# A two-layer diffusion backbone with eight experts: loading pairs of expert weight units only as pairs

## Chip, cores and metric

The kernel runs on one core of a Trainium2 chip. The metric is the device time of one execution in microseconds (us); the median of several runs is compared.

## What is computed

256 latent tokens and 256 context tokens of width 1024 pass through two layers: layer 0 is neighbourhood attention and a dense SwiGLU, layer 1 a two-way linear recurrence and a SwiGLU with eight experts, of which every token uses two. All inputs are fp32. The change touches the loading of the expert weights:

```python
def moe_ffn(h, w_router, b_router, w1, w3, w2):
    logits = (h @ w_router).astype(jnp.float32) + b_router.astype(jnp.float32)
    top_v, top_i = lax.top_k(logits, TOP_K)          # TOP_K = 2 of N_EXPERTS = 8
    gates = jax.nn.softmax(top_v, axis=-1)
    ...
    for e in range(N_EXPERTS):                       # D_FF_EXPERT = 3584
        y = y + comb[..., e:e + 1] * swiglu(h, w1[e], w3[e], w2[e])
```

Each expert has three matrices of 1024x3584 fp32, together 44 MB, and all eight are read once: 352 MB of the 490 MB that the whole kernel moves.

## The kernel before

**Units.** Weights come as units of 128x1024 fp32 (512 KB), in one list, in the order in which they are used. An expert is seven steps of 512 hidden columns. A step uses four units of w1, four of w3 (`up`, `small_up`) and, one step later, four of w2 (`w2_step`): 84 units an expert, 672 for all; only the last four (`w2c`, from `w2l`) are laid out otherwise. The host lays two neighbouring units side by side, so that a partition's 2x1024 values are 8 KB in one piece; the even unit of such a pair has a second way to be read, `both` (`add_moe`), which fetches the pair in one transfer of 1024 KB.

**Heavy and light experts.** Experts are sorted by their number of tokens. Places 0, 2, 4, 6 are heavy: ScalarE cuts each unit to a high part (`whi`, line 345), VectorE makes the low part (`wlo`, line 356), and TensorE does three matmuls of 512 columns for each product (lines 1871 to 1873 and 1804 to 1806). A heavy unit's place is free as soon as `wlo` is written. Places 1, 3, 5, 7 (`LIGHT`) have few tokens and use the raw fp32 units in TensorE (line 1784, called by `pair`); such a unit's place is free only when its matmuls are done.

**Places.** `Raws.homes` is a list of pools. Single places hold one unit (the pool `raw`, three of them; one more for a while), double places hold two (`wide`: four in `hp`, two in `rawm`, one in `raw3`, up to three in `zp`): 10 double and 3 single places for most of the expert stage. `load` is called whenever a place becomes free. It issues, on SyncE's queue (SP), as many loads as there are free places, strictly in the order of the list. A load waits on SP for the last reader of the place it writes. The expert's number is read from memory into a register of SP, since the order of the experts is data.

**How `load` chooses before.** If the next unit begins a pair and a double place is wholly free, it issues one transfer of 1024 KB (line 273). Otherwise it takes the first place that is free or half filled and issues the unit alone, 512 KB (line 289). A pair's first unit may thus fill a single place or the second half of a double place; the second unit of the pair has no `both` and is then always loaded alone, and it may open a double place whose other half the next pair's first unit fills. A double place is given back when both of its halves are used.

Of the kernel before, what the change touches and what calls it, by code (L numbers as in the profile page):

```python
# [241 lines left out]
class Raws:  # L242
# [18 lines left out]
    def add(self, key, ap, both=None):  # L261
        self.units.append((key, ap, both))

    def load(self, n=100):
        while self.dma_at < len(self.units) and n:
            n -= 1
            i = self.dma_at
            _, ap, both = self.units[i]
            r = next((r for r in self.homes if r.wide and r.free()), None) if both else None
            if r:  # L270
                b = r.block()
                b[1] = 2
                self.nc.sync.dma_start(b[0], both())
                self.raws[i], self.raws[i + 1] = (b[0][:, 0], b), (b[0][:, 1], b)
                self.dma_at += 2
                continue
            r = next((r for r in self.homes if r.part or r.free()), None)
            if r is None:
                return
            if r.part:  # L280
                b, t, r.part = r.part, r.part[0][:, 1], None
                b[1] += 1
            else:
                b = r.block()
                b[1] = 1
                t = b[0][:, 0] if r.wide else b[0]
                if r.wide:
                    r.part = b
            self.nc.sync.dma_start(t, ap() if callable(ap) else ap)
            self.raws[i] = (t, b)  # L290
            self.dma_at += 1

    def head(self):
        return self.units[self.at][0] if self.at < len(self.units) else None
# [100 lines left out]
def body(tc, nc, es, a, out, upto, dbg):  # L395
# [1548 lines left out]
    def overflow(p):  # L1944
# [38 lines left out]
        for s in range(NST):  # L1983
            acc = [psa("ph"), psa("ph")]
            for part in range(2):
                for i in range(4):
                    w = load(s, 4 * part + i)
                    for kk in range(2):
                        k = 2 * i + kk
                        nc.tensor.matmul(  # L1990
                            acc[part], xo[:, k], w[:, kk * 512:kk * 512 + 512], start=(k == 0), stop=(k == KD - 1)
                        )
            sil = mp.tile([P, 512], F32, name="msil", tag="msil", bufs=1)
            nc.scalar.activation(sil, acc[0], AF.Silu)
            nc.vector.tensor_tensor(sil, sil, acc[1], ALU.mult)
            g = pst("pgt")
            for i in range(4):
                nc.tensor.transpose(g[:, i * P:i * P + P], sil[:, i * P:i * P + P], ident)
            go = mp.tile([P, 512], F32, name="msil", tag="msil", bufs=1)
            nc.scalar.copy(go, g)  # L2000
            for f in range(4):
                w = load(s, 8 + f)
                for n in range(2):
                    nc.tensor.matmul(
                        yo[n], go[:, f * P:f * P + P], w[:, n * 512:n * 512 + 512],
                        start=(s == 0 and f == 0), stop=(s == NST - 1 and f == 3),
                    )
# [38 lines left out]
```

## Time and profile before

| | us |
|---|---|
| median of 3 runs | 1856.36 (1855.66 to 1859.17) |
| the profiled execution, its own time | 1857.41 |
| its span, first to last instruction | 1855.5 |
| TensorE busy | 1771.2 (95%) |
| VectorE busy | 1185.9 (64%) |
| ScalarE busy | 860.5 (46%) |
| chain that ended last: TensorE / DMA / VectorE | 71% / 13% / 10% |

The span is what the trace covers; 1.9 us of the execution's time lie around it. Busy time of TensorE counts matmuls whose ends are modelled, so 95% does not mean that it is at its limit everywhere. The 40 slices of the page are 46.4 us each; the expert stage begins in slice 22, counted from 1.

### The profile page before, as it was taken

What the parts mean: (1) busy time and instruction counts of PE and PEld (TensorE: products, weight loads), DVE (VectorE), ACT (ScalarE), POOL (GpSimd) and SP (SyncE); (2) the same over time, 40 slices, a digit from 0 to 9 for tenths busy, and PEclk for the clock granted to TensorE, in tenths of its full rate; (3) what the DMA queues carried; (4) which work ended last, traced back from release to release, by engine and by line L of the source; (5) the groups of instructions that cost most, each with busy time, mean ns of one, the idle gap of its engine ahead of it and who ended that gap; (6) DMA issues with size and microseconds to landing.
All of it is one profiled execution on the core that took longest, in us unless ns stands there. A gap on an engine that the chain in (4) does not pass through costs nothing.

```text
span 1855.5 us, 27189 instructions
## 1 busy us (share of the span) xinstructions
PE 1771.2 (95%) x10067; PEld 1351.2 (73%) x10067; DVE 1185.9 (64%) x1751; ACT 860.5 (46%) x1263; POOL 188.4 (10%) x195
## 2 busy tenths in 40 slices
PE   8999999999999999999778999999998999999996
PEld 6886568988788888877667885578655886478753
DVE  4784676877665447699988862288515972089611
ACT  4534655422222235776736761277314762067500
POOL 1001342100000002344640000000000000000000
PEclk8999999999999999999888999999999999999999
DMA  7444611464655223232566889999999999999996
GB/s 304 162 158 137 217 46 46 164 219 156 232 210 185 96 79 117 80 111 85 214 253 212 325 300 406 412 412 414 416 414 412 412 414 410 413 410 412 414 414 270
DMA packets 118588, 489.96 MB, mean 264 GB/s; under 512 B 13104, under 2 KB 18608, under 8 KB 100528
## 3 DMA queue, kind: packets, MB, share of 16 engines
q1 hardware_dynamic: 118304, 488.02, 69.1%
q8 instruction: 81, 1.33, 0.3%
q14 instruction: 59, 0.48, 0.1%
q10 hardware_dynamic: 144, 0.13, 0.0%
HBM read 487.05 MB, written 1.05 MB: 263 GB/s over the span
## 4 chain that ended last, share of the span: by engine, by line
PE 71%; DMA 13%; DVE 10%; ACT 3%; issue 1%; POOL 1%; SPq 0%; DVEq 0%; ACTq 0%; POOLq 0%
DMA raw<-moe_d 12%; PE ph L1784 6%; PE ph L1873 5%; PE ph L1871 5%; PE ph L1872 5%; PE psa L445 4%; PE psa L446 4%; PE psa L447 4%; PE py L1804 3%; PE py L1806 3%; PE py L1805 3%; PE py L1784 3%; DVE wlo L356 2%; PE pF L445 2%; PE pF L446 2%; PE pF L447 2%
## 5 line engine op out<-in xcount | busy, mean ns | idle before, releaser
L356 DVE TENSOR_TENSOR wlo<-raw,whi 128x1024 fp32r<-128x1024 f32 x480 | 575.4, 1234 | 158.1 <-ACT whi L345 154.7
L345 ACT CAST whi<-raw 128x1024 fp32r<-128x1024 f32 x484 | 491.5, 1048 | 207.0 <-PE pF L446 49.8
L1784 PE MATMUL ph<-raw,xs 128*64 128x256 f32 x1792 | 210.2, 383 | 9.1 <-DMA raw<-moe_d 8.8
L1873 PE MATMUL ph<-wlo,xe 128*128 128x512 f32 x448 | 177.3, 396 | 6.9 <-DVE wlo L356 6.8
L1871 PE MATMUL ph<-whi,xe 128*128 128x512 f32 x448 | 179.4, 400 | 2.2 <-ACT whi L345 2.2
L1784 PEld LDWEIGHTS ph<-raw,xs 128*64 128x64 f32 x1792 | 122.5, 137 | 76.3 <-DMA raw<-moe_d 13.6
L1872 PE MATMUL ph<-whi,xe 128*128 128x512 f32 x448 | 176.2, 393 | 0.0
L445 PE MATMUL psa<-hh,whi 128*128 128x512 f32 (+1 forms) x384 | 144.7, 377 | 0.0
L446 PE MATMUL psa<-hl,whi 128*128 128x512 f32 (+1 forms) x384 | 143.7, 374 | 0.7 <-DVE hl L696 0.6
L447 PE MATMUL psa<-hh,wlo 128*128 128x512 f32 (+1 forms) x384 | 143.2, 373 | 0.0
L1901 DVE TENSOR_TENSOR msil<-msil,ph 128x256 f32<-128x256 f32 x28 | 11.8, 420 | 155.7 <-PE ph L1784 155.7
L1784 PE MATMUL py<-raw,mgs 128*64 128x512 f32 (+1 forms) x496 | 104.6, 557 | 3.9 <-DMA raw<-moe_d 3.3
L1873 PEld LDWEIGHTS ph<-wlo,xe 128*128 128x128 f32 x448 | 85.2, 190 | 28.7 <-DVE wlo L356 10.3
L570 DVE SCALAR_TENSOR_TENSOR macc<-raw,c,macc 128x1024 f32<-128x1024 f32 x84 | 105.2, 1279 | 0.6
L1871 PEld LDWEIGHTS ph<-whi,xe 128*128 128x128 f32 x448 | 85.0, 190 | 19.2 <-ACT whi L345 2.9
L1872 PEld LDWEIGHTS ph<-whi,xe 128*128 128x128 f32 x448 | 85.3, 190 | 17.0
L1804 PE MATMUL py<-whi,mgh 128*128 128x512 f32 x224 | 87.6, 391 | 0.0
L1806 PE MATMUL py<-wlo,mgh 128*128 128x512 f32 x224 | 87.3, 390 | 0.0
L1805 PE MATMUL py<-whi,mgl 128*128 128x512 f32 x224 | 87.2, 389 | 0.0
L445 PEld LDWEIGHTS psa<-hh,whi 128*128 128x128 f32 x384 | 73.0, 190 | 14.3 <-issue 2.1
L446 PEld LDWEIGHTS psa<-hl,whi 128*128 128x128 f32 x384 | 73.0, 190 | 13.7 <-DVE hl L696 1.5
L447 PEld LDWEIGHTS psa<-hh,wlo 128*128 128x128 f32 x384 | 72.9, 190 | 12.5
(351 smaller groups left out, 3231.8 us busy)
## 6 DMA issues: line engine op xcount, KB each, us to landing
raw<-moe_d SPq DMA_DIRECT2D x388, 512.0 KB, 10.8
raw<-moe_d SPq DMA_DIRECT2D x140, 1024.0 KB, 14.1
raw<-f_d SPq DMA_DIRECT2D x66, 512.0 KB, 3.6
raw<-wm_d SPq DMA_DIRECT2D x64, 512.0 KB, 4.6
raw<-wmh_d SPq DMA_DIRECT2D x32, 512.0 KB, 7.5
raw<-qkv_d SPq DMA_DIRECT2D x24, 512.0 KB, 4.2
raw<-win_d SPq DMA_DIRECT2D x24, 512.0 KB, 3.6
raw<-gat_d SPq DMA_DIRECT2D x14, 512.0 KB, 3.7
```

The costliest lines, as they stand in the source:

```text
L345: self.nc.scalar.copy(hi, self.raws[i][0])
L356: eng.tensor_tensor(lo, self.take(key), hi.bitcast(F32), ALU.subtract)
L445: nc.tensor.matmul(o, w[0], x[0], start=first, stop=False)
L446: nc.tensor.matmul(o, w[0], x[1], start=False, stop=False)
L447: nc.tensor.matmul(o, w[1], x[0], start=False, stop=last)
L1784: nc.tensor.matmul(o[h], x, w[h], start=first, stop=last, skip_group_check=True)
L1804: nc.tensor.matmul(ys[e][n], x[0], w[0], start=b, stop=False)
L1805: nc.tensor.matmul(ys[e][n], x[1], w[0], start=False, stop=False)
L1806: nc.tensor.matmul(ys[e][n], x[0], w[1], start=False, stop=l)
L1871: nc.tensor.matmul(acc[part], xh[:, k], w[0], start=(k == 0), stop=False)
L1872: nc.tensor.matmul(acc[part], xl_[:, k], w[0], start=False, stop=False)
L1873: nc.tensor.matmul(acc[part], xh[:, k], w[1], start=False, stop=(k == 7))
```

## The change

`load` no longer breaks up a pair. A unit that begins a pair goes, with its partner, into a free double place in one transfer (now line 289); if there is none, both go at once into two free single places, as two transfers (`put`, line 276); if there are no two single places either, nothing is loaded until there is room. Half-filled double places are left to units that belong to no pair. The rest of the program is the same text nine lines further down.

```diff
+    def put(self, r):
+        i = self.dma_at
+        ap = self.units[i][1]
+        if r.part:
+            b, t, r.part = r.part, r.part[0][:, 1], None
+            b[1] += 1
+        else:
+            b = r.block()
+            b[1] = 1
+            t = b[0][:, 0] if r.wide else b[0]
+            if r.wide:
+                r.part = b
+        self.nc.sync.dma_start(t, ap() if callable(ap) else ap)
+        self.raws[i] = (t, b)
+        self.dma_at += 1
+
     def load(self, n=100):
         while self.dma_at < len(self.units) and n:
             n -= 1
             i = self.dma_at
-            _, ap, both = self.units[i]
-            r = next((r for r in self.homes if r.wide and r.free()), None) if both else None
-            if r:
+            both = self.units[i][2]
+            r = next((r for r in self.homes if r.wide and r.free()), None)
+            if both and r:
                 b = r.block()
                 b[1] = 2
                 self.nc.sync.dma_start(b[0], both())
                 self.raws[i], self.raws[i + 1] = (b[0][:, 0], b), (b[0][:, 1], b)
                 self.dma_at += 2
                 continue
-            r = next((r for r in self.homes if r.part or r.free()), None)
-            if r is None:
+            free = [r for r in self.homes for _ in range(1 if r.part else r.limit - r.used)]
+            if both:
+                free = [r for r in free if not r.wide]
+            if len(free) < (2 if both else 1):
                 return
-            if r.part:
-                b, t, r.part = r.part, r.part[0][:, 1], None
-                b[1] += 1
-            else:
-                b = r.block()
-                b[1] = 1
-                t = b[0][:, 0] if r.wide else b[0]
-                if r.wide:
-                    r.part = b
-            self.nc.sync.dma_start(t, ap() if callable(ap) else ap)
-            self.raws[i] = (t, b)
-            self.dma_at += 1
+            self.put(free[0])
+            if both:
+                self.put(free[1])
```

The order of the instructions of TensorE, VectorE, ScalarE and GpSimd stays as it was. SP's queue changes, from the first expert load on. In the rows below `raw_` and a number is one place's filling, 128x1024 one unit and 128x2048 a pair.

The first expert loads on SP before:

```order
L289 DMA raw_8131<-moe_d 128x1024
L289 DMA raw_8228<-moe_d 128x1024 x2
L289 DMA raw_8234<-moe_d 128x1024
L273 DMA raw_8236<-moe_d 128x2048
L289 DMA raw_8234<-moe_d 128x1024
L289 DMA raw_8243<-moe_d 128x1024 x2
L289 DMA raw_8326<-moe_d 128x1024 x2
L289 DMA raw_8407<-moe_d 128x1024 x2
```

And the same place in the changed program (line 289 is now the pair's line):

```order
L289 DMA raw_8226<-moe_d 128x2048
L289 DMA raw_8231<-moe_d 128x2048
L289 DMA raw_8233<-moe_d 128x2048
L289 DMA raw_8239<-moe_d 128x2048
L289 DMA raw_8321<-moe_d 128x2048
L289 DMA raw_8401<-moe_d 128x2048
```

Twelve units that came as one pair and ten single loads now come as six pairs, and the first of them stands where the second unit's load stood.

SP before, a little later, in the weights of the first expert (the loads go on like this):

```order
L273 DMA raw_9179<-moe_d 128x2048
L273 DMA raw_8596<-moe_d 128x2048
L273 DMA raw_8597<-moe_d 128x2048
L289 DMA raw_8600<-moe_d 128x1024
L289 DMA raw_9276<-moe_d 128x1024 x2
L289 DMA raw_9299<-moe_d 128x1024 x2
L289 DMA raw_9323<-moe_d 128x1024 x2
L289 DMA raw_9346<-moe_d 128x1024 x2
```

And in the changed program:

```order
L276 DMA raw_9112<-moe_d 128x1024
L276 DMA raw_9114<-moe_d 128x1024
L289 DMA raw_9137<-moe_d 128x2048
L289 DMA raw_8585<-moe_d 128x2048
L289 DMA raw_8586<-moe_d 128x2048
L276 DMA raw_9214<-moe_d 128x1024
L276 DMA raw_8589<-moe_d 128x1024
L289 DMA raw_9248<-moe_d 128x2048
L289 DMA raw_9270<-moe_d 128x2048
```

Before, a run of pairs is followed by a long run (22 to 26 units) of single loads, two to a double place; now single loads come only in twos, into the single places. From the second expert on the changed queue repeats ten pairs and two single loads, 22 units, with one shorter turn of eight pairs. Over the expert stage 140 pairs and 388 single loads (and the four of `w2l`) become 302 pairs and 64 single loads (and the four).

## Rows read from the trace of the kernel before

**Rows 1.** The page's part 2: DMA share and rate in 40 slices.
```profile
DMA  7444611464655223232566889999999999999996
GB/s 304 162 158 137 217 46 46 164 219 156 232 210 185 96 79 117 80 111 85 214 253 212 325 300 406 412 412 414 416 414 412 412 414 410 413 410 412 414 414 270
```

**Rows 2.** SP's waits, 1130 to 1836 us: total us, times, longest.
```profile
SPq L289 <- DMA raw<-moe_d: 311.0, 287, 2.7
SPq L273 <- DMA raw<-moe_d: 110.4, 107, 2.0
SPq L273 <- PE ph L1784: 19.9, 18, 4.3
SPq L289 <- PE ph L1784: 10.2, 18, 1.5
```

**Rows 3.** SP's waits, 1003 to 1107 us (first expert).
```profile
SPq L289 <- DVE wlo L356: 45.1, 23, 9.5
SPq L273 <- DVE wlo L356: 40.0, 13, 11.3
```

**Rows 4.** TensorE in order of time, where experts begin: start, us, operation.
```profile
1107.46 1.73 PE L1784 MATMUL ph<-raw,xs 128*64 128x256 f32 x14
...
1195.27 0.44 PE L1845 MATMUL pgt<-con,msil 128*128 128x128 f32 x2
1195.47 0.48 PE L1871 MATMUL ph<-whi,xe 128*128 128x512 f32 x1
...
1316.34 1.95 PE L1784 MATMUL ph<-raw,xs 128*64 128x256 f32 x16
...
1409.03 0.50 PE L1871 MATMUL ph<-whi,xe 128*128 128x512 f32 x1 [0.90 <-ACT whi L345]
...
1530.27 1.95 PE L1784 MATMUL ph<-raw,xs 128*64 128x256 f32 x16
...
1625.43 0.50 PE L1871 MATMUL ph<-whi,xe 128*128 128x512 f32 x1 [1.29 <-ACT whi L345]
...
1746.57 1.73 PE L1784 MATMUL ph<-raw,xs 128*64 128x256 f32 x14
```

**Rows 5.** Packets, 1121 to 1836 us: number, MB, rate, how many are small.
```profile
DMA packets 63200, 295.11 MB, mean 413 GB/s; under 512 B 7019, under 2 KB 7019, under 8 KB 47401
```

**Rows 6.** Packets, 1166 to 1197 and 1344 to 1374 us.
```profile
DMA packets 3382, 12.70 MB, mean 410 GB/s; under 512 B 377, under 2 KB 377, under 8 KB 3290
...
DMA packets 3187, 12.34 MB, mean 411 GB/s; under 512 B 356, under 2 KB 356, under 8 KB 3007
```

**Rows 7.** Packets, 1142 to 1163 and 1377 to 1394 us.
```profile
DMA packets 1271, 8.80 MB, mean 419 GB/s; under 512 B 139, under 2 KB 139, under 8 KB 257
...
DMA packets 1105, 7.13 MB, mean 420 GB/s; under 512 B 125, under 2 KB 125, under 8 KB 346
```

**Rows 8.** Windows: stretch, engines' busy us (x), clock, DMA share, GB/s.
```profile
1075.00:1100.00 25.00, 25.00 (x122) 20.90 (x121) 19.39 (x18) 19.20 (x25) 0.00 (x0) 1.00 0.91 338
1100.00:1125.00 25.00, 25.00 (x163) 18.07 (x162) 11.21 (x13) 7.23 (x10) 0.00 (x0) 1.00 0.86 308
1125.00:1150.00 25.00, 25.00 (x183) 13.62 (x184) 5.15 (x13) 3.10 (x8) 0.00 (x0) 1.00 1.02 417
...
1107.00:1195.00 88.00, 88.00 (x639) 50.29 (x637) 17.07 (x35) 15.55 (x32) 0.00 (x0) 1.00 0.99 393
```

**Rows 9.** DMA issues, 1067 to 1095 us: count, KB, median us to landing.
```profile
raw<-moe_d SPq DMA_DIRECT2D x9, 1024.0 KB, 4.8
```

**Rows 10.** TensorE in order of time near the end.
```profile
1834.13 3.65 PE L1784 MATMUL py<-raw,mgs 128*64 128x512 f32 x16 [0.65 <-DMA raw<-moe_d]
...
1836.58 0.33 PEld L1784 LDWEIGHTS py<-raw,mgs 128*64 128x64 f32 x4 [0.53 <-DMA raw<-moe_d]
1837.72 0.20 PEld L1845 LDWEIGHTS pgt<-con,msil 128*128 128x128 f32 x2 [0.81 <-issue]
1837.72 0.44 PE L1845 MATMUL pgt<-con,msil 128*128 128x128 f32 x2
```

## Prediction, made before the changed kernel ran

> **What bounds the kernel now.** I read the 40 slices first, since a share over the whole span hides the stages. TensorE looks busy everywhere, but from slice 25 on the DMA engines are full, at 406 to 416 GB/s in every slice up to the 39th [rows 1]. So the last 730 us are a stretch in which transfers stand back to back. The second view is SP's own waits there: loads wait 287 and 107 times for an earlier expert load to land, 421 us in all, and for TensorE to free places only 30 us [rows 2]. The queue never lacks work, and a free place is not what it waits for. In the first expert it is the other way: each wait is for `wlo`, which frees a place [rows 3]; the places are full and the transfers run at what TensorE uses up.
>
> The third view asks whether TensorE could go faster if the weights came sooner: where each expert begins [rows 4]. Heavy ones last 120.9, 121.2 and 121.1 us, the same each time. Light ones last 88.0, 92.7 and 95.2 us. The first light expert starts with the places full, so 88.0 us is what TensorE needs; the next two are 4.7 and 7.2 us longer, and the last one takes 1837.72 - 1746.57 = 91.2 us up to its last transposes against 1195.27 - 1107.46 = 87.8, so 3.4 us [rows 4, 10]. Near the end TensorE waits for the landing of single units [rows 10]. So the transfers bound the end, but by a small margin: with weights that came at once TensorE would gain 4.7 + 7.2 + 3.4 = 15.3 us and no more.
>
> **The change part by part.**
>
> *Removed and added transfers.* In the loop of the experts 388 single loads become 64, and 140 pairs become 302. SP gets 162 issues fewer. SP itself waits 421 us for landings [rows 2], so its saved issue time is worth nothing. The other engines keep their instructions in the same order.
>
> *The rate of the transfers.* A single load moves 4 KB pieces, a pair 8 KB pieces. Two stretches with almost only single loads (377 and 356 packets are tiny, nearly all others are 4 KB) run at 410 and 411 GB/s [rows 6]; two with almost only pairs at 419 and 420 [rows 7]. That is 2.2%. From 1121 to 1836 us, 295.11 MB move at 295.11 / 715 = 412.7 GB/s; 47401 - 7019 = 40382 packets of 4 KB make 165 MB, 56% of it, in single loads [rows 5]. After the change two units of each 22 are single, 9%. By the two rates the mixture goes from 1 / (0.56/410.5 + 0.44/419.5) = 414.4 to 418.7 GB/s. The smaller price is 295.11/414.4 - 295.11/418.7 = 712.1 - 704.8 = 7.3 us. But the stretch really ran at 412.7, so 2.9 us go somewhere that the clean windows leave out; the number of transfers falls by a third here, and if what is lost goes with them, the price is 715 - 704.8 = 10.2 us. If all of the stretch ran at 420, it would be 715 - 702.6 = 12.4 us. I take 10.2, because it starts from the one row that covers the whole stretch; 7.3 and 12.4 stay for the range.
>
> The Trainium skill has a rule that speaks against this term: "DMA: Bandwidth & Descriptors", section Specifications, puts the smallest transfer for full line rate at 512 B. By it pieces of 4 KB and of 8 KB go equally fast and the term is nothing. The windows above do not agree.
>
> *Where the full stretch begins.* Before, the first light expert starts at 1107.46 and the rate is 308 GB/s from 1100 to 1125, then 417 [rows 8]. TensorE uses up a light pair in sixteen matmuls, some 1.8 us (fourteen take 1.73) [rows 4], so from about 1109.3 places come free every 1.8 us, sooner than a pair is moved, 1.0486 MB at 419.5 GB/s or 2.5 us. A pair that comes alone lands 4.8 us after its issue [rows 9]; the first lands at 1114.1, and the stream is closed from 1111.6 on. Up to 1125 that is 13.4 us at 419.5, 5.6 MB; the 8 us after 1100 give, at the 338 GB/s of the slice before [rows 8], 2.7 MB. Together 8.3 MB against 308 x 25 = 7.7 MB before, so 0.6 MB or 1.5 us gained. Against it stands that the ring of places is shorter: one of three single places now stands idle, 22 units instead of 23, and a pair must wait until both of its places are free. That is one unit to one pair less in hand at the moment when the queue turns from full to hungry, 1.25 to 2.5 us lost. I take the gain of 1.5, as the releases there come in pairs anyway, and keep +2.5 as the other end.
>
> *The fill.* From the first load to 1107 us the new rule only delays loads. What hides it is the full ring: in the first expert every load waits for a place [rows 3], so some twenty units lie ready. If that cover were gone, each late pair would cost its 4.8 us. Nothing else is behind a waiting pair on SP except later expert loads.
>
> *The end.* Before, units come singly and TensorE works on one while the next moves; at the end it waits 0.53 us, then does the last four of sixteen matmuls of `py` [rows 10]. As the last two now land together, about one unit's matmuls more (3.65 / 4 = 0.9 us) follow the last landing: +1.0 us.
>
> *Sum.* -10.2 - 1.5 + 1.0 = -10.7 us. TensorE allows 15.3, so it does not stop this. The profiled execution took 1857.41 us, 1.05 above the median of the runs; 1857.41 - 10.7 = 1846.7, and on the scale of the median 1845.7. I say **1846 us**.
>
> **The rivals.**
>
> *Size of pieces does not matter* (the rule above). Then the difference between the windows came from what else ran in them: the first window of pairs lies in a light expert, the first of single loads too, which speaks against it, and so do the second two, both in the next light expert. Only the beginning and the end move: -1.5 + 1.0 to +2.5 + 1.0, so 1856 to 1860, most likely 1856. Chance 0.09.
>
> *The ring runs full.* The transfers get ahead during a heavy expert: in 120.9 us at 418.7 GB/s they bring 96.5 units and TensorE takes 84. With about two units in hand at its start, 14.5 of 22 places are full at its end, and 7.5 units, 9.4 us, are under way; a lone pair needs 4.8 us [rows 9]. It holds by 3.6 units. SP's waits for line 1784 (30 us) show that this edge is touched today [rows 2]. If it does not hold, a pair comes alone once or more at each of three such places, 4.8 - 2.5 = 2.3 us each: some 7 us given back, 1853. Chance 0.08.
>
> *Pairs come one at a time in the first light expert* (the other side). That is how pairs ran from 1075 to 1100, at 338 GB/s [rows 8]. If waiting for both halves keeps the queue like this for the 88 us of the first light expert, which now moves 393 GB/s [rows 8], 88 x 55 = 4.8 MB or 11.6 us are lost. The gain of the rate is then left only on the later 627 of 715 us, 8.9 us: 1856.4 + 11.6 - 8.9 + 1.0 = 1860. It decides by whether places come free more slowly than a pair moves, 2.5 us; the 1.8 us above speak against it. Chance 0.06.
>
> **How the numbers follow.** My own case has 0.77. Its time is 1846; its bounds are -12.4 - 1.5 + 1.0 = -12.9 (1843.5) and -7.3 + 2.5 + 1.0 = -3.8 (1852.5). TensorE's bound of 15.3 would give 1841. The range 1841 to 1853 holds my case and the rival of the full ring, 0.85. A change under 0.2%, 3.7 us, cannot be told from none here. Faster by more than that: my case and a part of the full ring, 0.84. Within 0.2%: the equal rates, for the most part, and the rest of the full ring, 0.10. Slower: the lone pairs, 0.06.
>
> **What would show it.** In the profile after: 302 pairs in the list of issues; from about 1112 us on a rate near 418 GB/s instead of 413; heavy experts still 121 us, light ones nearer to 88; the first heavy expert after the light one beginning at the same 1195 us. Wrong would be: 413 GB/s as before (equal rates); stretches under 400 GB/s where a light expert begins, with SP waiting for line 1784's place (now 1793) for more than 30 us (full ring); or a first light expert that moves less than 393 GB/s (lone pairs).

## The result and the profile after

The changed kernel takes 1847.47 us, median of six runs (1843.97 to 1849.13), against 1856.38 for the kernel before in the same session (1854.33 to 1859.17): ratio 0.9949, 95% interval 0.9936 to 0.9962. That is 8.9 us or 0.5% faster. Two later sessions with the same program gave 1845.56 (ratio 0.9942, 0.9925 to 0.996) and 1846.78 (0.9945, 0.993 to 0.996). The forecast was 1846.

The profiled execution spans 1847.4 us, against 1855.5 before. I read the same views as before. First the 40 slices and the issues of expert weights over the whole kernel:

```profile
DMA  7444611464665323232565979999999999999996
GB/s 304 163 150 147 206 58 46 160 209 148 235 217 193 100 83 115 80 103 91 195 249 189 355 279 387 418 419 420 419 419 420 419 420 416 420 420 419 415 419 281
...
raw<-moe_d SPq DMA_DIRECT2D x302, 1024.0 KB, 15.3
raw<-moe_d SPq DMA_DIRECT2D x64, 512.0 KB, 15.7
```

302 pairs and 64 singles, as the order of the program said, and from the 26th slice on 415 to 420 GB/s, where [rows 1] had 410 to 416. The packets of the full stretch, 1121 to 1827 us, answer to [rows 5]:

```profile
DMA packets 44448, 295.61 MB, mean 419 GB/s; under 512 B 4936, under 2 KB 4936, under 8 KB 11857
```

11857 - 4936 = 6921 packets of 4 KB are left of 40382. The same bytes take 706 us instead of 715. SP's waits from 1130 to 1836 us answer to [rows 2]:

```profile
SPq L289 <- DMA raw<-moe_d: 208.1, 126, 2.7
SPq L289 <- DVE wlo L365: 123.4, 68, 3.7
SPq L289 <- PE ph L1793: 100.9, 59, 4.7
SPq L276 <- DMA raw<-moe_d: 51.9, 28, 2.7
```

Waits for an earlier landing fell from 421 to 260 us, and waits for a place to come free rose from 42 us (`ph` 30 in [rows 2], and 12 for `wlo` in the two rows of before that follow) to 224 in the two rows above:

```profile
SPq L289 <- DVE wlo L356: 7.1, 17, 2.2
SPq L273 <- DVE wlo L356: 5.2, 10, 2.0
```

Where the experts begin on TensorE, as [rows 4], and its end, as [rows 10]:

```profile
1110.05 5.18 PE L1793 MATMUL ph<-raw,xs 128*64 128x256 f32 x46
...
1198.08 0.48 PE L1880 MATMUL ph<-whi,xe 128*128 128x512 f32 x1
...
1317.54 1.73 PE L1793 MATMUL ph<-raw,xs 128*64 128x256 f32 x14
...
1408.48 0.50 PE L1880 MATMUL ph<-whi,xe 128*128 128x512 f32 x1 [1.26 <-ACT whi L354]
...
1529.63 1.73 PE L1793 MATMUL ph<-raw,xs 128*64 128x256 f32 x14
...
1620.02 0.50 PE L1880 MATMUL ph<-whi,xe 128*128 128x512 f32 x1 [1.27 <-ACT whi L354]
...
1741.15 1.08 PE L1793 MATMUL ph<-raw,xs 128*64 128x256 f32 x8
...
1827.21 1.94 PE L1793 MATMUL py<-raw,mgs 128*64 128x512 f32 x8 [0.48 <-DMA raw<-moe_d]
1829.08 0.44 PE L1854 MATMUL pgt<-con,msil 128*128 128x128 f32 x2
```

The first light expert begins 2.6 us later than before (1110.05 against 1107.46), yet the last transposes come 8.6 us earlier (1829.08 against 1837.72). So the change gains inside the expert stage, and something ahead of it lost a little. The second and third light expert last 90.9 and 90.4 us, before 92.7 and 95.2, and the last one takes 87.9 up to its last transposes, before 91.2. The three heavy experts between them last 119.5, 121.2 and 121.1 us, before 120.9, 121.2 and 121.1. From the start of the first light expert on, what TensorE still waits for, before (two rows) and then after (two rows):

```profile
PE ph L1784 <- DMA raw<-moe_d: 8.8, 13, 1.5
PE py L1784 <- DMA raw<-moe_d: 3.3, 10, 0.7
```

```profile
PE py L1793 <- DMA raw<-moe_d: 4.5, 7, 1.4
PE ph L1793 <- DMA raw<-moe_d: 1.4, 4, 0.6
```

12.1 us became 5.9: the transfers still bound the end.

**Where the 8 us came from.** From the DMA records of both traces I took when unit 107 (early in the full stretch) and unit 667 (the last of the ordinary ones) had landed. Before: 1120.73 and 1836.54, end 1855.54. After: 1123.21 and 1827.17, end 1847.35. Split at these points:

| stretch | before | after | difference |
|---|---|---|---|
| span's start to first light expert | 1107.46 | 1110.05 | +2.6 |
| first light expert to landing of unit 107 | 13.3 | 13.2 | -0.1 |
| landing of unit 107 to that of 667 | 715.8 | 704.0 | -11.9 |
| landing of unit 667 to the end | 19.0 | 20.2 | +1.2 |

(Differences are taken before rounding; their sum, -8.2, is the difference of the spans.) Between the two landings the kernel before moved 295.39 MB, 412.7 GB/s, and the changed one 294.74 MB, 418.7 GB/s. The rate alone makes 10.3 of the 11.9 us; the other 1.6 us are the 0.65 MB less, and why fewer bytes fall between the same two landings is open. From the first light expert to the end it is 748.1 us before and 737.3 after, 737.2 and 737.0 in the two later profiles. This figure leaves out what happens ahead of the experts, so it is the yardstick below, beside the medians.

### The profile page after: what moved, and what is told of

Read it like the earlier page. It is cut to its first block, busy times and chain, and to the rows that moved or that the text cites. A ratio compares the mean times of both kernels' runs of the same rounds, so it can differ in the third digit from the quotient of the medians.

```text
span 1847.4 us, 26663 instructions
## 1 busy us (share of the span) xinstructions
PE 1770.6 (96%) x10067; PEld 1357.1 (73%) x10067; DVE 1185.7 (64%) x1751; ACT 859.7 (47%) x1263; POOL 189.3 (10%) x195
## 4 chain that ended last, share of the span: by engine, by line
PE 76%; DVE 11%; DMA 8%; ACT 2%; issue 2%; POOL 1%; SPq 0%; DVEq 0%; ACTq 0%; POOLq 0%
PE ph L1793 8%; DMA raw<-moe_d 7%; PE ph L1882 5%; PE ph L1880 5%; PE ph L1881 5%; PE psa L454 4%; PE psa L455 4%; PE psa L456 4%; PE py L1793 3%; PE py L1813 3%; PE py L1815 3%; PE py L1814 3%; DVE wlo L365 2%; PE pF L454 2%; PE pF L455 2%; PE pF L456 2%
## 5 line engine op out<-in xcount | busy, mean ns | idle before, releaser
L1881 PEld LDWEIGHTS ph<-whi,xe 128*128 128x128 f32 x448 | 86.2, 192 | 17.3
L455 PEld LDWEIGHTS psa<-hl,whi 128*128 128x128 f32 x384 | 73.1, 190 | 13.6 <-DVE hl L705 1.5
## 6 DMA issues: line engine op xcount, KB each, us to landing
raw<-moe_d SPq DMA_DIRECT2D x302, 1024.0 KB, 15.3
```

Source lines behind the costliest of these rows:

```text
L455: nc.tensor.matmul(o, w[0], x[1], start=False, stop=False)
L1881: nc.tensor.matmul(acc[part], xl_[:, k], w[0], start=False, stop=False)
```

## Experiments

**What in a pair is faster: its long pieces or the smaller number of transfers?** My theory: mostly the 8 KB pieces, with a part for the number. The rivals: the number alone, or neither (only the order of the places counts). Four versions of the changed program keep its places and its order; they differ in how a pair comes into a double place.

`two_singles`: two transfers of 512 KB, 4 KB pieces.

```diff
-                self.nc.sync.dma_start(b[0], both())
+                w = both()
+                for h in range(2):
+                    self.nc.sync.dma_start(b[0][:, h], w[:, h])
```

> Same places and same moments as the changed kernel, but each double place is filled by two transfers of 512 KB with 4 KB pieces. Theory 'transfers' (larger ones move faster): the full stretch falls from 419 to about 410 GB/s, 295 MB take 719 instead of 704 us, so 1862 us, and up to 1870 if each transfer costs something of its own. Rival 'places' (the gain comes from not breaking pairs over places): 1847 us as the changed kernel.

`pair_4k`: one transfer of 1024 KB, but of 4 KB pieces: the host lays the two units behind each other instead of side by side.

```diff
-    twos = lambda w: w.reshape(NE, NST, 2, 2, P, UNIT).transpose(0, 1, 2, 4, 3, 5)
+    twos = lambda w: w.reshape(NE, NST, 2, 2, P, UNIT)
...
-        st.add(key, moe(p, q, j, slice(None), i % 2), None if i % 2 else moe(p, q, j))
+        st.add(key, moe(p, q, j, i % 2), None if i % 2 else lambda: moe(p, q, j)().rearrange("i p u -> p i u"))
...
-                nc.sync.dma_start(pair_[0], a["moe"][expert(p) if p else 0, s, i // 2])
+                nc.sync.dma_start(pair_[0], a["moe"][expert(p) if p else 0, s, i // 2].rearrange("i p u -> p i u"))
```

> Each double place is filled by one transfer of 1024 KB, but the pair is laid out as two units one behind the other, so the pieces are 4 KB. If the size of the pieces decides: 410 GB/s and 1860 us or more. If the number of transfers decides: 418 to 420 GB/s and 1847 to 1850 us.

`half_rows`: two transfers of 512 KB, 8 KB pieces, partitions 0 to 63 and then 64 to 127.

```diff
-                self.nc.sync.dma_start(b[0], both())
+                w = both()
+                for h in (slice(0, 64), slice(64, P)):
+                    self.nc.sync.dma_start(b[0][h], w[h])
```

> Each double place is filled by two transfers of 512 KB, each for 64 partitions with 8 KB pieces: as many transfers as with single loads, pieces as with pairs. If the size of the pieces decides: 418 to 420 GB/s and 1847 to 1850 us. If the number of transfers decides: about 410 GB/s and 1860 us or more.

`half_rows` told nothing on the number of transfers: it took 2451.15 us (ratio 1.3167, 1.3118 to 1.3216). Its window from 1200 to 2400 us:

```profile
1200.00:2400.00 1200.00, 838.19 (x3576) 484.06 (x3576) 369.57 (x400) 305.07 (x379) 0.00 (x0) 0.87 1.01 227
```

The DMA engines are busy all the time (share 1.01) at 227 GB/s: something that only this choice of partitions brings. So I made it again with halves that each reach over all partitions.

`alt_rows`: two transfers of 512 KB, 8 KB pieces, the even partitions and then the odd ones.

```diff
-                self.nc.sync.dma_start(b[0], both())
+                w = both()
+                for h in range(2):
+                    self.nc.sync.dma_start(b[0][h::2], w[h::2])
```

> Like half_rows, but each of the two transfers takes every second partition, so that both spread over all 128. Pieces of 8 KB, 668 expert transfers. In the run before, the two halves of the partitions one after the other gave only 227 GB/s, so that run told nothing about the number of transfers. Sum of two terms (pieces of 4 KB cost 17 us over the full stretch, each transfer more costs 0.017 us): 704 + 5 us, so 1851 us. If the number of transfers costs nothing: 1846 us. If half of the partitions is slow however they are chosen: over 2400 us again.

`changed_again`: the changed kernel itself beside the first three of these.

> The changed kernel once more, as the base of this group and for a second profile. All theories: about 1847 us, ratio to before 0.993 to 0.996. The stretch before the first light expert differs between the two profiles by 2.6 us at a granted clock that fell at another moment; if that is chance, the first light expert should begin anywhere from 1107 to 1111 us here; if the change causes it, again near 1110.

The packets from 1125 to 1827 us, in the order `changed_again`, `alt_rows`, `pair_4k`, `two_singles`:

```profile
DMA packets 44211, 293.85 MB, mean 419 GB/s; under 512 B 4908, under 2 KB 4908, under 8 KB 11841
```

```profile
DMA packets 48140, 292.95 MB, mean 417 GB/s; under 512 B 8915, under 2 KB 8915, under 8 KB 15917
```

```profile
DMA packets 74706, 286.93 MB, mean 409 GB/s; under 512 B 4771, under 2 KB 4771, under 8 KB 74656
```

```profile
DMA packets 78475, 286.26 MB, mean 408 GB/s; under 512 B 8712, under 2 KB 8712, under 8 KB 78419
```

| version | transfers of units | pieces | median us | ratio to before | unit 107 to 667 |
|---|---|---|---|---|---|
| `changed_again` | 366 | 8 KB | 1845.56 | 0.9942 (0.9925 to 0.996) | 703.6 |
| `alt_rows` | 668 | 8 KB | 1851.61 | 0.9974 (0.9962 to 0.9985) | 708.6 |
| `pair_4k` | 366 | 4 KB | 1863.24 | 1.0042 (1.0027 to 1.0058) | 720.9 |
| `two_singles` | 668 | 4 KB | 1869.95 | 1.0069 (1.0051 to 1.0086) | 726.1 |

The two causes add up. 4 KB pieces cost 720.9 - 703.6 = 17.3 us with few transfers and 726.1 - 708.6 = 17.5 with many; the greater number costs 5.0 us with 8 KB pieces and 5.2 with 4 KB. Each of these figures is from one profile; three profiles of the changed kernel give 704.0, 703.6 and 703.1 us. The medians agree within their scatter: 17.7 and 18.3 us for the pieces, 6.1 and 6.7 for the number (`alt_rows` is from a later session). Both rivals fall: pieces and number each have a price, and with the number at its lowest `pair_4k` is still slower than the kernel before. As both versions with 4 KB have the changed order of places, that order alone is not what gains. These two read the units from different layouts in memory, so the layout isn't the cause either. Pieces of half the length are also twice as many, and no run separates the two.

The change makes only a part of each step, and I take its share of each price as proportional. From the first light expert on, before had 319 single loads and 123 pairs, after 52 and 257; `two_singles` has 566 single loads there. So the pieces change in 257 - 123 = 134 pairs of 257, 134/257 x 17.4 = 9.1 us, and the number falls by 442 - 309 = 133 of 566 - 309 = 257, 133/257 x 5.1 = 2.6 us. Together 11.7 us, where the stretch gained 11.9.

**How far would TensorE go?** The forecast let TensorE gain 15.3 us and no more. To test this, the last of the three matrices is not fetched for the light experts, so that the transfers cannot bind.

```diff
-                for i in range(4):
+                for i in range(0 if pe in LIGHT else 4):
...
-            u = st.need(("w2", e, s, f))
+            u = hn_h[:, f % 2].bitcast(F32) if e in LIGHT else st.need(("w2", e, s, f))
...
-            st.done(("w2", e, s, f))
+            if e not in LIGHT:
+                st.done(("w2", e, s, f))
```

> Leaves out the loading of w2 for the four light experts, but for the four last units: their matmuls run as before, on rows that lie in SBUF for another use. 112 units, 59 MB, are not moved; TensorE's work is the same. If TensorE is close behind the transfers, light experts take 88.0 us each and heavy ones 121, and the time is 1839 to 1843 us. If the transfers alone set the end: 140 us less, 1706 us.

It took 1829.36 us (ratio 0.9852, 0.9829 to 0.9876), 27 us below before and 10 below the lower end expected. (It leaves out 108 units, 56.6 MB; the 112 of the expectation count the four last ones in.) The starts of its light experts:

```profile
1106.53 7.13 PE L1793 MATMUL ph<-raw,xs 128*64 128x256 f32 x64
...
1313.23 1.95 PE L1793 MATMUL ph<-raw,xs 128*64 128x256 f32 x16
...
1519.94 1.30 PE L1793 MATMUL ph<-raw,xs 128*64 128x256 f32 x10
...
1726.65 1.73 PE L1793 MATMUL ph<-raw,xs 128*64 128x256 f32 x14
...
1808.51 0.44 PE L1855 MATMUL pgt<-con,msil 128*128 128x128 f32 x2
```

A light and a heavy expert together take 206.7 us every time, and no wait of TensorE for a landing is left. With the 88.0 us of a light expert, a heavy one needs 118.7, not the 121 of [rows 4]; and the last light expert needs 1808.51 - 1726.65 = 81.9, not 87.8. So there was more to be had than the forecast's cap: 748.1 us from the first light expert to the end before, 719.3 here, 28.8 in all.

**Does the ring of places run full?** The forecast's rival says that the transfers get ahead in a heavy expert until no place is free. After the change SP did wait 224 us for places, and yet the rate did not fall. `ring18` takes two double places away, 18 units instead of 22.

```diff
-            if n == (1, 7):
-                st.widen(zr, 2)
...
-    st.widen(zr, 3)
```

> The changed kernel with two double places fewer: 18 units instead of 22 go round. If the places in hand are not needed: 1846 us. If the stock at the moment when the transfers become the bound counts, each missing unit costs its 1.25 us once: 5 us, 1851 us. If the ring also runs full where each of three heavy experts ends (7.5 units under way would become 3.5, 4.4 us against the 4.8 of a lone pair): 7 us more, up to 1858 us, and stretches under 400 GB/s near 1317, 1529 and 1740.

1857.11 us, ratio 1.0 (0.9985 to 1.0015): the whole gain is gone. Just before and just after its second light expert begins:

```profile
1290.00:1320.00 30.00, 30.00 (x138) 24.85 (x137) 26.23 (x26) 21.85 (x24) 0.00 (x0) 1.00 1.01 419
1320.00:1345.00 25.00, 25.00 (x174) 17.54 (x174) 9.95 (x13) 6.88 (x10) 0.00 (x0) 1.00 0.96 377
```

The rate drops to 377 GB/s in the place that the rival named, and its 40 slices show 396 and 390 where the second and third light expert begin:

```profile
GB/s 303 162 159 136 211 52 46 160 217 156 231 212 184 100 80 124 80 103 94 215 212 170 304 342 391 419 419 420 396 419 419 419 418 390 419 419 419 412 419 299
```

With 22 units the lowest slice of the full stretch is 415. So the rival's mechanism exists, and 22 units are enough; where between 18 and 22 they cease to be enough, no run shows. From the first light expert on `ring18` takes 746.1 us, 2 less than before. Unit 107 lands 17.6 us after that expert's start, 4.4 later than with 22 units, 1.1 us for each unit that is missing; from there to unit 667 it takes 709.2 us, 5 to 6 more than the changed kernel.

`ring24` goes the other way: a fourth single place, for which small tiles share space; now all single places can be used in twos, 24 units. For the same space a further single place, ahead of the experts, is filled once instead of twice (`AG`).

```diff
-AG = (1,1)
+AG = (1,0)
...
+                st.add_pool(pool(ms, "raw4", 1, side="right"), 1)
...
-            small["P"] = mp.tile([P, 2, 4, CAP], F32R, name="Ps", bufs=1)
+            small["P"] = mp.tile([P, 2, 4, CAP], F32R, name="Ps", tag="ysb", bufs=1)
...
-            pc = mp.tile([P, 2, P], F32, name="Pm", tag="Pd", bufs=1)
+            pc = mp.tile([P, 2, P], F32, name="Pm", tag="Pm", bufs=1)
...
-            gt = mp.tile([P, 2, 2, CAP], F32, name="mgs", tag="mgs", bufs=2)
+            gt = mp.tile([P, 2, 2, CAP], F32, name="mgs", tag="mgs", bufs=1)
...
-        spot = mp.tile([P, 2, P], F32, name="spot", tag="Pd", bufs=1)
+        spot = mp.tile([P, 2, P], F32, name="spot", tag="Pm", bufs=1)
```

> One single place more (room is made by letting small tiles share memory), so four single places hold two pairs and 24 units go round instead of 22; no engine's order changes but SP's. With 18 units the stretch of full rate began 6 us later, 1.5 us a unit. If the stock still counts above 22: 3 us earlier, less some 1.5 us as 4 of 24 units instead of 2 of 22 now come in 4 KB pieces: about 1.5 us faster than the changed kernel in the same call. If 22 is enough: 1 to 2 us slower than it.

`changed_third`: the changed kernel once more, beside `ring24`.

> The changed kernel as base of this group and for a third profile: 1845 to 1848 us. If the later begin of the first light expert (1110 us in two profiles, 1107 before) is chance of the granted clock, it may begin at 1106 to 1108 here; if it belongs to the change, at 1110 again.

`ring24` took 1844.18 us (1842.96 to 1849.82), `changed_third` 1846.78 (1844.16 to 1847.63); ratios 0.9939 (0.9921 to 0.9956) and 0.9945 (0.993 to 0.996). The intervals overlap, so it isn't shown to be faster. (The 6 us in the expectation of `ring24` are counted from the span's start, and 1.6 of them are the later start of the first light expert in `ring18`.) In the profile of `ring24` unit 107 lands 10.8 us after the first light expert's start, 13.6 in `changed_third`; but it has more single loads (110 against 64), and the units from 107 to 667 take 705.8 us against 703.1. From the first light expert to the end it is 736.0 against 737.0 us: what is gained at the start is mostly given back in the stretch, where the single loads are. A still longer ring wasn't tried.

**The end.** `last_single` fetches only the last pair of the ordinary units singly.

```diff
+        last = key[:3] == ("w2", NE - 1, NST - 2) and i > 1
-        st.add(key, moe(p, q, j, slice(None), i % 2), None if i % 2 else moe(p, q, j))
+        st.add(key, moe(p, q, j, slice(None), i % 2), None if i % 2 or last else moe(p, q, j))
```

> The changed kernel, with the last pair of w2 before the four last units loaded as two single units. By the prediction's term for the end the last pair costs 1.0 us: 1845.5 us instead of 1846.5, and 19.1 us instead of 20.2 from the landing of the last pair's second unit to the end. If the term is nothing: no difference.

```profile
1824.58 0.30 PEld L1794 LDWEIGHTS py<-raw,mgs 128*64 128x64 f32 x4 [0.56 <-DMA raw<-moe_d]
...
1825.69 0.20 PEld L1855 LDWEIGHTS pgt<-con,msil 128*128 128x128 f32 x2 [0.81 <-issue]
```

From the last wait to the transposes it is 1.1 us, as in [rows 10] before (1836.58 to 1837.72), and 1.9 after the change (1827.21 to 1829.08). The step is there, 0.7 us. It did not reach the end: from the landing of unit 667 to the end of the span it is 20.0 us, where 19.1 was expected and the three profiles of the changed kernel have 20.2 to 20.4. From the transposes to VectorE's last instruction it is 11.4 us before, after and here; what differs is the stretch behind it, in which the output is stored. It takes 6.4 us before, 6.8 after and 7.4 here, and 6.0 in `ring24`. The median, 1847.78 (1846.35 to 1851.78; ratio 0.9954, 0.9936 to 0.9972), is no lower than the changed kernel's: so small a gain can't be told from the scatter of the runs.

No version here is shown to beat the changed kernel.

**The 2.6 us ahead of the experts.** Two profiles of the same changed program start the first light expert at 1110.05 and 1110.18 us, a third at 1108.00. Windows of the first and of `changed_third`:

```profile
982.00:1000.00 18.00, 18.00 (x71) 14.63 (x71) 11.92 (x21) 11.26 (x13) 0.00 (x0) 0.85 0.49 180
```

```profile
982.00:1000.00 18.00, 17.50 (x80) 14.16 (x79) 14.36 (x38) 12.97 (x16) 0.00 (x0) 1.00 0.60 233
```

The mean granted clock of 0.85 says that TensorE ran for a part of the window at 1.2 GHz; in `changed_third`, as in the kernel before, it is 1.00, the level of 2.4 GHz, throughout. TensorE had been idle for a fifth to a quarter of the time from 965 to 975 us in all of them. The first heavy expert, which begins near 982 us in all of them, lasts 128.1 us in the first profile, 126.0 in `changed_third` and 126.0 before. The same program shows both, so this difference needs no change of the program. Why it goes one way or the other stays open, and so does whether the change makes the longer one likelier: there is one profile of before only, and the medians moved by 8.9 to 10.3 us, less than the 10.8 to 11.1 from the first light expert on.

## Why the prediction was right

**The bound.** It was right that the transfers bind from the first light expert on, and that their rate sets the end: the rate rose and the stretch got shorter by the same amount.

**The rate, -10.2 us (7.3 from the pieces, 2.9 from the number of transfers).** This term carried the forecast; it measured -11.9 between the landings, 10.3 by the mean rates, and the experiments put 9.1 on the pieces and 2.6 on the number. The choice to trust the row of the whole stretch (412.7 GB/s) over the clean windows was right, and the rate after it, 418.7, is the one forecast. The reason given was wrong. The windows do not leave out the number of transfers: those with single loads [rows 6] have the short pieces and the greater number at once. They were a little better, at 410 and 411 GB/s, than single loads are over the whole stretch (408 in `two_singles`). With that rate the mixture of before comes to 1 / (0.56/408 + 0.44/419) = 412.8, the measured 412.7, and nothing of the rate is left over for another cause. That 2.6 us for the number came out near the 2.9 of the forecast is luck.

**Equal rates.** The rival fell: 4 KB pieces cost 17 us of 704 with the number of transfers unchanged. So the rule of the Trainium skill, "DMA: Bandwidth & Descriptors", section Specifications, that 512 B are enough for full rate, does not hold here to the last per cent. The same page of the Trainium skill, section "Why small descriptors are slow (HBM only)", tells of a fixed cost of some three cycles for each packet beside one for each 32 B. As an estimate by that cost alone, 8 KB against 4 KB would gain (131/128) / (259/256) - 1 = 1.2%; the runs show 17.4 us of 704, 2.5%, twice as much.

**The begin of the full stretch, -1.5 us.** This step failed, at the sentence "I take the gain of 1.5". It measured -0.1. Both parts that the prediction weighed were there and cancelled. The first 18 us of the first light expert, before and then after:

```profile
1107.50:1125.50 18.00, 18.00 (x132) 12.36 (x131) 7.37 (x9) 5.81 (x8) 0.00 (x0) 1.00 0.87 317
1110.00:1128.00 18.00, 18.00 (x132) 12.38 (x130) 7.37 (x9) 5.80 (x8) 0.00 (x0) 1.00 0.86 342
```

That is 25 x 18 = 0.45 MB more, 1.1 us. But up to that expert's start 189.38 MB had come before and 189.00 after, 0.38 MB or 0.9 us less in hand. A unit of ring is worth 1.1 to 1.2 us (18, 22 and 24 units: 17.6, 13.2 and 10.8 us), so the one place that stands idle accounts for the loss. The mean of the two ends (-1.5 and +2.5) would have been nearer.

**The end, +1.0 us.** It is 0.7 us up to the transposes, by the mechanism named (the last two units land together), and 1.2 from the landing of unit 667 to the end of the span. The other 0.5 lies behind VectorE's last instruction, in a stretch that takes 6.0 to 7.4 us in the profiles, so the runs do not show it to be the change.

**Sum.** -11.9 - 0.1 + 1.2 = -10.8 against the forecast's -10.7, and with the +2.6 ahead of it the -8.2 of the spans; the medians moved by -8.9, -10.3 and -9.1 in the three sessions. The total is nearer than its terms, and that is luck: the rate gave 1.7 more, the begin 1.4 less. For the stage ahead of the light expert the forecast put nothing (*The fill*); the three profiles of the changed kernel are 0.5, 2.6 and 2.7 us later than the one of before.

**The cap, 15.3 us "and no more".** It was mis-sized; TensorE had 28.8 us to gain. The yardsticks were wrong: heavy experts that all last 121 us looked like a limit, but each was still 2.4 us short of it (three of them, 7.1 us), and the last light expert was measured by the first, which takes 5.9 us more with its weights at hand. It did no harm, as the transfers stopped the gain earlier, but it set the lower end of the range.

**The sign for a full ring.** Of its two halves, "SP waiting for line 1784's place for more than 30 us" came true (100.9 us, and 123.4 for `wlo`) while the rate stayed at 419. This half was no sign: SP's wait for a place cost nothing, as other transfers were still queued on the DMA engines (a pair landed 15.3 us after its issue in the median, and 2.5 us are enough to move it). The other half, the rate at the light experts' starts, was the right sign, and `ring18` shows how it looks. By the working the rival stood 3.6 units off at 22, and with four units less it came.

**Lone pairs.** The rival fell: the first light expert moved 402 GB/s, not less than the 393 of [rows 8]:

```profile
1110.00:1198.00 88.00, 88.00 (x637) 50.10 (x636) 17.56 (x35) 16.12 (x33) 0.00 (x0) 1.00 0.98 402
```

It lasted 88.0 us as before, so the heavy expert behind it began 2.6 us later (1198.08 against 1195.47) for no reason but its start.

## What to carry to other kernels

Where transfers stand back to back, two per cent in the rate of one kind against another can be worth more than the waits of the queue that issues them: read the rate of clean windows of each kind, but take the size of the term from the row of the whole stretch. Length of pieces and number of transfers are two prices, and a version that changes one alone separates them. An engine that takes the same time in each turn isn't thereby at its limit; to learn the limit, take the load away that could bind.

## What the runs showed of the hardware that was not expected

Two transfers to partitions 0 to 63 and 64 to 127, one after the other, run at 227 GB/s with all DMA engines busy, while two transfers to the even and the odd partitions run at 417: by that choice alone the kernel takes 2451.15 or 1851.61 us. The Trainium skill, "SBUF — State Buffer", section "Door 1: The DMA port swizzle", has the first half of it: partitions 0 to 63 reach only half of the ports. By its section "Can I just issue two DMAs to hit both halves?" a second transfer to the other half is hardly carried beside the first. The trace agrees: 227 is 54% of 417. That halves of interleaved partitions lose nothing but the price of the number of transfers, the runs here add.

Where transfers were always queued, one more transfer for the same bytes cost 5.1 / 257 = 0.02 us. A pair that came alone landed 4.8 us after its issue [rows 9], 2.3 more than the 2.5 that it took in the queue.
